# Keys' stage of a hybrid encoder step: more places for token tiles, evictions and raw weights, in memory given up by the dynamic DMAs' reserve

## The chip, the cores and the metric

The kernel runs on one core of a Trainium2 chip. The metric is device time in microseconds (us), the median of three runs. TensorE (PE) multiplies and transposes, VectorE (DVE) and ScalarE (ACT) evict and normalise, GpSimd (POOL) takes subtractions that would load DVE, and the SP queue issues every DMA of this kernel. Each engine, SP's queue included, takes its instructions in the order in which they were written down.

## The reference

One layer of a streaming encoder on 16 meta tokens, 2048 prompt tokens and 8 x 16 sample tokens. Cut to what matters here:

```python
h = layer_norm(concat([meta, x_prompt]), ln_in_g, ln_in_b)      # the samples likewise
(g_q, g_k, g_v, g_low, g_r, d_q, d_k, d_v, i_q, i_k, i_w, d_z, m_a, m_b) = split(h @ w_in)
o_a, s_t = gla_recurrence(q, k, v, log_f, s0)                    # gated linear attention
k_i = layer_norm(i_k, idx_kn_g, idx_kn_b)                        # keys of the indexer
o_b = attend(d_q, i_q, w_i, d_k, d_v, k_i)                       # top 256 keys by index score, then softmax
merged = sigmoid(m_a + gate_b[0]) * y_a + sigmoid(m_b + gate_b[1]) * y_b
h_new = layer_norm(ALPHA * h + merged @ w_out, ln_g, ln_b)
```

The keys d_k, values d_v, index keys k_i and the final state are outputs as well.

## The kernel before

Every float32 operand of a large product is split in two halves, a rounded one (`xh`, `whi`, written by ACT) and the remainder (`xl`, `wlo`, written by DVE or POOL). `mm3` (lines 265 to 267) takes three matmuls for each of eight steps of 128 along the model width, in the order hi x hi, hi x lo, lo x hi.

**Keys' stage** (`phase_keys`) goes through 18 token tiles: the meta tokens (16 rows), 16 prompt tiles of 128 rows and one tile of samples. They lie in six pieces of three tiles. For each tile `rows_in` loads x (512 KB, line 271), `prep_x` takes the LayerNorm on DVE (statistics at line 181, two steps at line 153), stores the result to `d_h` (line 283), transposes it with eight PE instructions (line 288), splits it into `xh` and `xl` (lines 159 and 144) and, for the four pieces that have to be read again later, copies it to `xf` and stores it to `d_xt` (lines 293, 294). One tile later `keys` multiplies it with two weight blocks of 300 columns (48 matmuls), evicts K (`kd`), V (`vt`) and the index columns (`xi`), transposes the keys (line 335), splits them into `ks`, and after a `yield` normalises the index keys into `xd` and transposes them (lines 349, 350). The weights come in quarters through `raw` tiles.

**Buffers.** A tile asked for by name gets the next of its pool's places and waits until the last reader of that place is done. x has three places (pool `iqp`), the evicted tiles `kd`, `vt`, `ks`, `xf` share four places of 2 KB (pool `ev`), `xi`, `xd`, `gl` four small ones (tag `evs`), `raw` has three.

**Order.** The program does not fix the order in which an engine takes its work. A list scheduler walks the program with priorities and a timeline of its own and writes one order per engine. When a place comes free at another time on that timeline, rows change places, far from the buffer that changed too.

**Afterwards.** `project` runs three groups of pieces through the remaining columns of w_in, with index scoring (line 445) and the choice of keys on DVE beside it. `phase2` then opens its own pools in the same memory: from the left the lower end (keys of the upper half, GLA pools), from the right end attention's pools (`lg`, `v`, `kdl1`, `az`, `pts`, `sm`, `st`, `aq`, `kdl0`, `up`). A pool of phase 2 can be written when the tiles of phase 1 at the same addresses are done. Attention (logits at lines 1129 and 1130, evicted by DVE at line 1131 into `lgl` and `lgu` with the row maxima `mx` in pool `sm`; transposes at 1065; product with V at 1089) is interleaved with side work: the samples' attention (lines 1182 to 1225) and the GLA recurrence (lines 682 to 960).

The memory is bounded by the reserve that the program object keeps for dynamic DMAs. Before, it has its default size, and the kernel's own tiles begin 16512 bytes into each partition.

Of the kernel before, what the change touches and what calls it, by code (L numbers as in the profile page):

```python
# [10 lines left out]
F32 = mybir.dt.float32  # L11
# [10 lines left out]
P = 128  # L22
# [21 lines left out]
KLOW = 1040  # L44
HALF = 8
LAST = [(7, 0), (6, 2), (5, 1), (0, 1), (4, 2), (2, 1), (1, 1), (3, 0)]
NP3 = 256
EARLY = 1500
SKB = 3
# [33 lines left out]
PMAX = 3 * P  # L83
# [36 lines left out]
class Trunk:  # L120
# [108 lines left out]
        return full[META + t * P : META + (t + 1) * P, :]  # L229

    def raw(self, n):
        t = self.ws.tile([P, 2 * PMAX], F32, name="raw", bufs=3)
        return t[:, : 2 * n].rearrange("p (k c) -> p k c", k=2)

    def split_sb(self, hi, lo, src, eng=None):
# [77 lines left out]
    def keys(self, t, x, c, w1, w2):  # L313

        nc, d, c0 = self.nc, self.d, COL[t]
# [8 lines left out]
        nc.sync.dma_start(self.out_rows("k", t, 256).rearrange("t (g d) -> t g d", g=4), kd[:r, :, 0, :])  # L324
        nc.sync.dma_start(self.out_rows("v", t, 256), vt[:r])
        nc.sync.dma_start(d["v"][c0 : c0 + r, :], vt[:r])
        xi = self.ev.tile([P, 80], F32, name="xi", tag="evs", bufs=4)
        nc.scalar.copy(xi[:r, 0:64], p2[:, 212:276])
        nc.scalar.copy(xi[:r, 64:80], p2[:, 284:300])
        if t != "m":  # L330
# [10 lines left out]

        mu, rstd = self.ln_stats(self.tk, xi[:r, 0:64], 64, r)
        self.stt(xi[:r, 0:64], xi[:r, 0:64], mu, self.ing[:r], OP.subtract, OP.mult)
        xd = self.ev.tile([P, 2, 64], F32, name="xd", tag="evs", bufs=4)
        for q in range(2):
            self.stt(xd[:r, q, :], xi[:r, 0:64], rstd, self.inb[:r], OP.mult, OP.add)
        nc.sync.dma_start(self.out_rows("idx_k", t, 64), xd[:r, 0, :])
# [2 lines left out]
        nc.tensor.transpose(ps[:16, 1, :r], xi[:r, 64:80], self.ident[:r, :r])  # L350
        kc = NKEY if t == "s" else (0 if t == "m" else META + t * P)
        self.split(self.kih[:, kc : kc + r], self.kil[:, kc : kc + r], ps[:, 0, :r])
        gl = self.ev.tile([16, P], F32, name="gl", tag="evs", bufs=4)
        nc.scalar.copy(gl[:, :r], ps[:16, 1, :r])
        nc.sync.dma_start(d["gl"][:, c0 : c0 + r], gl[:, :r])

# [203 lines left out]
    def phase1(self):  # L560
        nc, tc, i = self.nc, self.tc, self.i
        with ExitStack() as c:
            top = tc.tile_pool(name="top", bufs=1, side="right")
            top = c.enter_context(top)
            kp = c.enter_context(tc.tile_pool(name="kp", bufs=1))
            self.scp = c.enter_context(tc.tile_pool(name="scp", bufs=4))
            self.iqp = c.enter_context(tc.tile_pool(name="iqp", bufs=3))
            self.tk = c.enter_context(tc.tile_pool(name="tk", bufs=4))
            self.jk = c.enter_context(tc.tile_pool(name="jk", bufs=1))
            self.xp = [c.enter_context(tc.tile_pool(name=f"xp{q}", bufs=1)) for q in range(3)]  # L570
            self.ev = c.enter_context(tc.tile_pool(name="ev", bufs=4))
            self.ws = c.enter_context(tc.tile_pool(name="ws", bufs=2))
            self.pi = c.enter_context(tc.tile_pool(name="pi", bufs=4, space=PSUM))
            self.pp = c.enter_context(tc.tile_pool(name="pp", bufs=4, space=PSUM))
            self.kih = kp.tile([P, NKEY + P], F32R, name="kih")
            self.kil = kp.tile([P, NKEY + P], F32R, name="kil")
            self.iw = kp.tile([P, NT, 8], F32, name="iw")
            self.ing = self.bcast_load(kp, i["idx_kn_g"][0], 64, "ing")
            self.inb = self.bcast_load(kp, i["idx_kn_b"][0], 64, "inb")
            self.x, self.slots = {}, [0, 1, 2, 0, 1, 2, 0, 1, 2, 1]  # L580
            self.phase_keys()
            self.gng = self.bcast_load(top, i["gla_norm_g"][0], 256, "gng")
            self.gateb = top.tile([P, 16], F32, name="gateb")
            nc.sync.dma_start(self.gateb[:], i["gate_b"][0].rearrange("a (k p) -> p (a k)", p=P))
            for g in range(len(GROUPS)):
                self.project(g)
# [669 lines left out]
    def phase2(self):  # L1256
        nc, tc, d = self.nc, self.tc, self.d
        with ExitStack() as main:
# [63 lines left out]
            next(steps)  # L1322
            for j, n in LAST:
                for _ in self.attend(j):
# [165 lines left out]
```

## Time and profile before

| what | value |
|---|---|
| median of three runs | 3597.57 us (3590.15 to 3598.61) |
| profiled execution | 3593.96 us |
| its span on the core | 3592.2 us |
| PE, DVE, ACT, POOL busy in the span | 3483.6, 2528.4, 1450.9, 1088.8 us |
| DMA | 457.77 MB, mean 127 GB/s |

The span is the time from the first to the last instruction of the profiled execution. Busy times of engines overlap. In the rows further down, an instruction's idle time before it stands in square brackets, with the instruction or the DMA that ended it, and the granted clock is a share of full speed: at 1.00 PE runs at 2.4 GHz.

### The profile page before, as it was taken

How to read it: one execution, taken by the hardware profiler on the slowest of the kernel's cores; microseconds unless marked ns; L12 is line 12 of the kernel's file. 1: busy time of each engine (PE TensorE's matmuls, PEld its weight loads, DVE VectorE, ACT ScalarE, POOL GpSimd, SP SyncE). 2: the span in 40 equal slices, each digit the busy share in tenths (PEclk: the TensorE clock that was granted, in tenths of full speed). 3: DMA queues.
4: the chain of work that ended last, by engine and by line, in shares of the span. 5: the costliest groups of instructions: out<-in, count | busy, mean ns of one | idle time of the engine just before them, and what ended most of it. 6: DMA issues, size and time to landing. Idle time of an engine off the chain costs nothing. (4 is left out here: it accounts for less than half of the span.)

```text
span 3592.2 us, 66024 instructions
## 1 busy us (share of the span) xinstructions
PE 3483.6 (97%) x24196; PEld 3212.5 (89%) x24196; DVE 2528.4 (70%) x5813; ACT 1450.9 (40%) x3092; POOL 1088.8 (30%) x1412
## 2 busy tenths in 40 slices
PE   7999999999999998999999999999999999989999
PEld 6999999999999998998887788888877888879998
DVE  7737998799999998964436677676765666544444
ACT  4435223433324323322535556566565344331110
POOL 3122242242342334434411345455410000022221
PEclk9999999999999999999999999999999999999999
DMA  8642443254442345445573433333343345564431
GB/s 265 202 131 82 139 121 108 83 157 127 119 145 73 103 134 148 140 134 159 171 199 94 122 109 97 102 105 99 100 121 88 89 120 135 151 192 136 124 115 62
DMA packets 550340, 457.77 MB, mean 127 GB/s; under 512 B 95248, under 2 KB 522528, under 8 KB 550016
## 3 DMA queue, kind: packets, MB, share of 16 engines
q1 hardware_dynamic: 550016, 453.56, 43.9%
q8 instruction: 190, 3.11, 0.4%
q14 instruction: 134, 1.10, 0.1%
HBM read 292.49 MB, written 160.92 MB: 126 GB/s over the span
## 5 line engine op out<-in xcount | busy, mean ns | idle before, releaser
L144 POOL TENSOR_TENSOR wlo<-raw,whi 128x512 fp32r<-128x512 f32 x360 | 482.3, 1360 | 817.1 <-ACT whi L159 706.7
L150 DVE TENSOR_SCALAR_CACHE_REDUCE junk<-sc,cand 128x272 bf16<-128x272 f32 (+6 forms) x512 | 701.6, 1370 | 16.9
L265 PE MATMUL pp<-whi,xh 128*128 128x256 f32 (+3 forms) x1952 | 562.1, 288 | 3.5 <-ACT whi L159 2.3
L265 PE MATMUL pp<-xh,whi 128*128 128x384 f32 (+2 forms) x1728 | 563.6, 326 | 1.9 <-ACT whi L159 1.1
L267 PE MATMUL pp<-whi,xl 128*128 128x256 f32 (+3 forms) x1952 | 560.8, 288 | 4.4 <-DVE xl L144 4.4
L267 PE MATMUL pp<-xh,wlo 128*128 128x384 f32 (+2 forms) x1728 | 563.0, 327 | 1.0 <-POOL wlo L144 1.0
L266 PE MATMUL pp<-xl,whi 128*128 128x384 f32 (+2 forms) x1728 | 563.4, 326 | 0.0
L266 PE MATMUL pp<-wlo,xh 128*128 128x256 f32 (+3 forms) x1952 | 561.9, 288 | 0.0
L265 PEld LDWEIGHTS pp<-whi,xh 128*128 128x128 f32 (+1 forms) x1952 | 371.9, 191 | 12.7 <-issue 4.3
L267 PEld LDWEIGHTS pp<-whi,xl 128*128 128x128 f32 (+1 forms) x1952 | 371.0, 190 | 11.3 <-DVE xl L144 6.9
L266 PEld LDWEIGHTS pp<-wlo,xh 128*128 128x128 f32 (+1 forms) x1952 | 371.5, 190 | 7.8 <-issue 5.2
L1131 DVE CUSTOM_DVE_ANT_0 lgl<-pl,mkl 128x348 f32<-128x348 f32 (+8 forms) x608 | 296.1, 510 | 102.8 <-PE pl L1130 65.8
L265 PE MATMUL pd<-xh,wh 128*128 128x242 f32 (+3 forms) x1152 | 327.7, 285 | 8.2 <-ACT wh L1347 4.5
L159 ACT CAST whi<-raw 128x512 fp32r<-128x512 f32 (+1 forms) x344 | 199.2, 622 | 319.7 <-DMA raw<-in_w_in 204.8
L265 PEld LDWEIGHTS pp<-xh,whi 128*128 128x128 f32 x1728 | 325.1, 188 | 3.3 <-ACT whi L159 1.7
L267 PEld LDWEIGHTS pp<-xh,wlo 128*128 128x128 f32 x1728 | 324.8, 188 | 2.5 <-POOL wlo L144 1.8
L266 PE MATMUL pd<-xl,wh 128*128 128x242 f32 (+3 forms) x1152 | 324.6, 282 | 2.1 <-DVE xl L144 2.1
L266 PEld LDWEIGHTS pp<-xl,whi 128*128 128x128 f32 x1728 | 325.1, 188 | 0.6
L267 PE MATMUL pd<-xh,wl 128*128 128x242 f32 (+3 forms) x1152 | 324.5, 282 | 0.8 <-POOL wl L144 0.8
L156 ACT ACTIVATE lgl<-lgl,mx 128x1040 f32<-128x1040 f32 (+7 forms) x256 | 249.9, 976 | 177.9 <-DVE mx L1133 171.4
L1129 PE MATMUL pl<-kd,q 128*128 128x348 f32 (+14 forms) x800 | 302.5, 381 | 14.1 <-DVE mx L1131 4.9
L1130 PE MATMUL pl<-kd,q 128*128 128x348 f32 (+14 forms) x800 | 261.7, 330 | 0.0
(252 smaller groups left out, 7592.7 us busy)
## 6 DMA issues: line engine op xcount, KB each, us to landing
raw<-in_w_in SPq DMA_DIRECT2D x360, 256.0 KB, 3.2
q<-d_q SPq DMA_DIRECT2D x272, 128.0 KB, 3.0
d_h<-x SPq DMA_DIRECT2D x17, 512.0 KB, 3.3
d_gv<-en SPq DMA_DIRECT2D x68, 128.0 KB, 1.9
d_gr<-en SPq DMA_DIRECT2D x68, 128.0 KB, 2.0
d_z<-en SPq DMA_DIRECT2D x68, 128.0 KB, 1.7
v<-d_gv SPq DMA_DIRECT2D x17, 512.0 KB, 3.7
gr<-d_gr SPq DMA_DIRECT2D x17, 512.0 KB, 3.6
```

The lines of the kernel that those rows point to most:

```text
L144: (eng or self.nc.vector).tensor_tensor(out, a, b, op=op)
L150: (eng or self.nc.vector).tensor_scalar(out, a, s1, s2, op0=op0, op1=op1, **kw)
L156: self.nc.scalar.activation(out, a, f, **kw)
L159: (self.nc.vector.tensor_copy if self.spare else self.nc.scalar.copy)(out, src)
L265: mm(ps, ah(k), bh(k), start=k == 0, stop=False)
L266: mm(ps, ah(k), bl(k), start=False, stop=False)
L267: mm(ps, al(k), bh(k), start=False, stop=k == n - 1)
L1129: nc.tensor.matmul(ps[:, :m], q[:, u, :], kd, start=True, stop=False)
L1130: nc.tensor.matmul(ps[:, :m], q[:, 2 + u, :], kd, start=False, stop=True)
L1131: nc.vector.tensor_tensor_reduce(lg[z1][:, a : a + m], ps[:, :m], mk[z1][:, a : a + m], 1.0, NEG, OP.add, OP.max, mx[:, s : s + 1])
```

## The change

The reserve of the dynamic DMAs is set to 1024 bytes, and the tiles of the kernel begin 15360 bytes earlier. The room is used in phase 1: pool `iqp` has four places for x (4 KB more), `ev` seven in place of four (6 KB), the tag `evs` eight in place of four (2 KB), and `raw` four in place of three (3 KB). No instruction is added or removed; on every engine the same instructions stand in another order.

```diff
+DMA_SCRATCH = 1024
@@ raw
-        t = self.ws.tile([P, 2 * PMAX], F32, name="raw", bufs=3)
+        t = self.ws.tile([P, 2 * PMAX], F32, name="raw", bufs=4)
@@ keys
-        xi = self.ev.tile([P, 80], F32, name="xi", tag="evs", bufs=4)
+        xi = self.ev.tile([P, 80], F32, name="xi", tag="evs", bufs=8)
-        xd = self.ev.tile([P, 2, 64], F32, name="xd", tag="evs", bufs=4)
+        xd = self.ev.tile([P, 2, 64], F32, name="xd", tag="evs", bufs=8)
-        gl = self.ev.tile([16, P], F32, name="gl", tag="evs", bufs=4)
+        gl = self.ev.tile([16, P], F32, name="gl", tag="evs", bufs=8)
@@ phase1
-            self.iqp = c.enter_context(tc.tile_pool(name="iqp", bufs=3))
+            self.iqp = c.enter_context(tc.tile_pool(name="iqp", bufs=4))
-            self.ev = c.enter_context(tc.tile_pool(name="ev", bufs=4))
+            self.ev = c.enter_context(tc.tile_pool(name="ev", bufs=7))
@@ kernel
-    nc = bacc.Bacc("TRN2", target_bir_lowering=False, num_devices=1)
+    nc = bacc.Bacc("TRN2", target_bir_lowering=False, num_devices=1, dynamic_dma_scratch_size=DMA_SCRATCH)
```

In the order rows below, lines of the changed kernel are one higher than those of the profile. The first place is SP's queue at the start of the kernel. Before (a number tells the tiles of one name apart):

```order
L256 DMA raw_165<-in_w_in 128x2x300
L256 DMA raw_169<-in_w_in 128x2x300
L256 DMA raw_173<-in_w_in 128x2x300
L271 DMA x_338<-in_x_prompt 128x1024
L190 DMA gng_2373<-in_gla_norm_g 128x256
L584 DMA gateb_2375<-in_gate_b 128x16x1
L271 DMA x_462<-in_x_prompt 128x1024
L283 DMA d_h_75<-x_159 128x1024
L256 DMA raw_177<-in_w_in 128x2x300
L256 DMA raw_183<-in_w_in 128x2x212
```

And in the changed kernel, from the same row on:

```order
L257 DMA raw_165<-in_w_in 128x2x300
L257 DMA raw_169<-in_w_in 128x2x300
L257 DMA raw_173<-in_w_in 128x2x300
L257 DMA raw_177<-in_w_in 128x2x300
L272 DMA x_338<-in_x_prompt 128x1024
L272 DMA x_462<-in_x_prompt 128x1024
L191 DMA gng_2373<-in_gla_norm_g 128x256
L585 DMA gateb_2375<-in_gate_b 128x16x1
L272 DMA x_584<-in_x_prompt 128x1024
L284 DMA d_h_75<-x_159 128x1024
L257 DMA raw_183<-in_w_in 128x2x212
```

The fourth quarter of the first weight block (raw_177) and one more x tile stand ahead of the first row that waits for a place; the x loads after that stand about one tile earlier throughout the stage.

The second place is DVE ahead of the meta tile's `xd`. Before:

```order
L153 SCALAR_TENSOR_TENSOR x_584<-x_584,mv_589,lnb_156 128x1024
L181 BN_STATS st_708<-x_706 128x6
L183 BN_AGGR mv_443<-st_441 16x2
L183 BN_AGGR mv_711<-st_708 128x2
L148 TENSOR_SCALAR mv_443<-mv_443 16x1
L153 SCALAR_TENSOR_TENSOR xi_326<-xi_326,mv_443,ing_151 16x64
L148 TENSOR_SCALAR mv_711<-mv_711 128x1
L153 SCALAR_TENSOR_TENSOR x_706<-x_706,mv_711,lng_155 128x1024
L181 BN_STATS st_565<-xi_428 128x6
L144 TENSOR_TENSOR ks_437<-pk_432,ks_437 64x512
L183 BN_AGGR mv_567<-st_565 128x2
L153 SCALAR_TENSOR_TENSOR xd_448<-xi_326,mv_443,inb_153 16x64 x2
```

After (st_832, the statistics of x_830, stands two rows above the first of these):

```order
L154 SCALAR_TENSOR_TENSOR x_706<-x_706,mv_711,lng_155 128x1024
L184 BN_AGGR mv_443<-st_441 16x2
L184 BN_AGGR mv_835<-st_832 128x2
L182 BN_STATS st_565<-xi_428 128x6
L154 SCALAR_TENSOR_TENSOR x_706<-x_706,mv_711,lnb_156 128x1024
L149 TENSOR_SCALAR mv_443<-mv_443 16x1
L154 SCALAR_TENSOR_TENSOR xi_326<-xi_326,mv_443,ing_151 16x64
L149 TENSOR_SCALAR mv_835<-mv_835 128x1
L154 SCALAR_TENSOR_TENSOR x_830<-x_830,mv_835,lng_155 128x1024
L184 BN_AGGR mv_567<-st_565 128x2
L145 TENSOR_TENSOR ks_437<-pk_432,ks_437 64x512
L154 SCALAR_TENSOR_TENSOR xd_448<-xi_326,mv_443,inb_153 16x64 x2
```

The statistics and the first step of x_830 and the second step of x_706 now stand ahead of xd_448.

The third place is the handover from the projections to attention. PE before, from the last keys of the samples on (kd_21349 is the first half of the lower keys, kd_20308 an upper one):

```order
L1182 MATMUL pg<-ident,kn 128x128 x4
L1129 MATMUL pl<-kd_21349,q 128x348
L1130 MATMUL pl<-kd_21349,q 128x348
L1129 MATMUL pl<-kd_21349,q 128x348
L1130 MATMUL pl<-kd_21349,q 128x348
L1129 MATMUL pl<-kd_21349,q 128x344
L1130 MATMUL pl<-kd_21349,q 128x344
L1182 MATMUL pg<-ident,kn 128x128 x4
L1129 MATMUL pl<-kd_20308,q 128x512
L1130 MATMUL pl<-kd_20308,q 128x512
```

PE after:

```order
L1130 MATMUL pl<-kd_21349,q 128x344
L1131 MATMUL pl<-kd_21349,q 128x344
L1205 MATMUL pg<-ident,slg 128x128
L1210 MATMUL pg<-ident,slg 16x128
L1205 MATMUL pg<-ident,slg 128x128 x3
L1210 MATMUL pg<-ident,slg 16x128
L1217 MATMUL pg<-vn,pn 128x128
L1219 MATMUL pg<-vb,spt 128x128 x2
L1217 MATMUL pg<-vn,pn 128x128
L1219 MATMUL pg<-vb,spt 128x128 x2
L1225 MATMUL pg<-ident,on 128x128
L1183 MATMUL pg<-ident,kn 128x128 x8
```

After the third pair of logits PE now takes the rest of one block of sample attention and then a whole second one before the first logits with kd_20308. DVE there, after:

```order
L1195 ISA slg,smx<-pg,smk 128x272
L1195 ISA smx 128x1
L1161 CAST qsl<-q 128x4x32
L1161 CAST qsh<-q 128x4x32
L1161 CAST qsl<-q 128x4x32
L149 TENSOR_SCALAR smx<-smx 128x2
L1199 RECIPROCAL smx<-smx 128x2
L145 TENSOR_TENSOR zs<-zg,smx 128x128
L1132 ISA lgl,mx<-pl,mkl 128x348
```

The last of these rows is DVE's first logit; before, that row stood ahead of the split of the next sample keys. On SP the load of kd_21349 stood before in one place with that of kd_21351, just ahead of the last two query stores; now it stands eight rows further ahead, and kd_21351 where both were. In memory, kdl0 (the place of kd_21349) lay over pools xp1 and xp2 and lies over xp2 alone, which holds the piece whose last matmuls come first; pool sm lay over xp2 and lies over the fourth and fifth eviction places.

## Rows read from the trace of the kernel before

**Rows 1.** The page: busy us, share of the span and instructions, by engine.

```profile
PE 3483.6 (97%) x24196; PEld 3212.5 (89%) x24196; DVE 2528.4 (70%) x5813; ACT 1450.9 (40%) x3092; POOL 1088.8 (30%) x1412
```

**Rows 2.** Stretches: length; PE, PEld, DVE, ACT, POOL busy (instructions); PE's clock; DMA share; GB/s.

```profile
12.50:50.00 37.50, 31.99 (x199) 27.79 (x200) 31.35 (x55) 16.85 (x43) 13.58 (x11) 0.91 0.91 260
50.00:140.00 90.00, 83.74 (x614) 80.47 (x613) 73.67 (x160) 43.73 (x134) 23.76 (x24) 1.00 0.85 259
140.00:150.00 10.00, 10.00 (x79) 9.98 (x77) 8.12 (x20) 4.15 (x16) 1.98 (x2) 1.00 0.79 244
...
1850.00:1950.00 100.00, 87.76 (x577) 70.50 (x576) 57.38 (x195) 51.88 (x107) 16.64 (x32) 0.95 0.53 142
1950.00:2700.00 750.00, 732.10 (x5066) 608.15 (x5065) 520.52 (x1847) 445.38 (x960) 323.83 (x627) 1.00 0.38 107
```

**Rows 3.** Waits of PE, 0 to 170 us: total us, times, longest us.

```profile
PE pt L288 <- DVE x L153: 12.5, 1, 12.5
PE pp L267 <- DVE xl L144: 4.4, 6, 1.2
PE pk L349 <- DVE xd L153: 3.2, 1, 3.2
PE pp L265 <- ACT whi L159: 2.3, 2, 1.4
PE pp L265 <- ACT xh L159: 1.0, 4, 0.2
PE pk L335 <- DVE ks L144: 0.9, 1, 0.9
```

**Rows 4.** Groups of DVE, 50 to 140 us: busy us, mean ns | idle before, releaser.

```profile
L153 DVE SCALAR_TENSOR_TENSOR x<-x,mv,lnb 128x1024 f32<-128x1024 f32 x10 | 13.2, 1316 | 0.9 <-POOL mv L144 0.7
...
L181 DVE BATCH_NORM_STATS2 st<-x 128x6 f32<-128x512 f32 x20 | 12.8, 684 | 10.0 <-DMA x<-in_x_prompt 10.0
L153 DVE SCALAR_TENSOR_TENSOR x<-x,mv,lng 128x1024 f32<-128x1024 f32 x10 | 12.8, 1276 | 0.0
```

**Rows 5.** Waits of SP's queue, 0 to 170 us, at line 271 (x loads).

```profile
SPq L271 <- PE pp L267: 7.2, 4, 2.0
...
SPq L271 <- DVE x L153: 5.2, 1, 5.2
```

**Rows 6.** PE in order of time: start us, duration us, instruction, idle before.

```profile
22.35 0.45 PE L266 MATMUL pp<-wlo,xh 128*128 128x300 f32 x1
22.60 0.45 PE L267 MATMUL pp<-whi,xl 128*128 128x300 f32 x1
...
26.05 0.30 PE L266 MATMUL pp<-wlo,xh 128*16 128x300 f32 x1
26.18 0.30 PE L267 MATMUL pp<-whi,xl 128*16 128x300 f32 x1
...
45.88 1.97 PE L288 MATMUL pt<-ident,x 128*128 128x128 f32 x8
...
54.36 1.04 PE L288 MATMUL pt<-ident,x 128*128 128x128 f32 x8
```

**Rows 7.** The page: DMA queue and kind, packets, MB, share of 16 engines.

```profile
q1 hardware_dynamic: 550016, 453.56, 43.9%
```

**Rows 8.** PE at the handover, in order of time.

```profile
1860.53 0.48 PE L1216 MATMUL pg<-vn,pn 16*128 16x128 f32 x2 [0.82 <-ACT pn L1211]
...
1863.49 0.30 PE L1224 MATMUL pg<-ident,on 128*128 128x128 f32 x1 [0.78 <-DVE on L144]
...
1866.89 0.66 PE L1129 MATMUL pl<-kd,q 128*128 128x348 f32 x1 [2.62 <-DMA kd<-d_kd]
```

**Rows 9.** SP's queue at the handover: the loads of the lower keys.

```profile
1859.09 0.89 SPq L172 DMA_DIRECT2D kd<-d_kd  x2
```

**Rows 10.** ACT at the handover: keys split and softmax of a sample block.

```profile
1864.31 0.59 ACT L1184 CAST ks<-pg 128x512 fp32r<-128x512 f32 x1 [0.22 <-PE pg L1182]
...
1878.43 0.50 ACT L156 ACTIVATE slg<-slg,smx 128x272 f32<-128x272 f32 x1
```

**Rows 11.** Waits of PE, 1950 to 2700 us, the largest: total, times, longest us.

```profile
PE pg L754 <- DVE og L153: 3.3, 7, 0.9
```

## Prediction

> **What bounds the kernel now.** I read the engine line of the page first: TensorE (PE) is busy for 3483.6 of 3592.2 us [rows 1]. So only about 109 us of waiting can be won anywhere, and the question is how much of it lies where the change acts. The table by stage [rows 2] answers that. In it I subtract PE's busy time from the width of each stretch. Keys' stage runs from PE's first instruction at 12.5 us to about 140 us; from there on PE has 10.00 us of work in 10, since projection matmuls fill every gap. PE loses 37.5 - 31.99 = 5.5 us there before 50 us and 90 - 83.74 = 6.3 us after it. Two other places matter below: 12.2 us in 1850 to 1950 (the handover from projections to attention) and 17.9 us in the 750 us of attention that follow. The first reading is therefore that the whole of Keys' stage can give back 11.8 us of idle PE, a third of a percent, before anything is said about what the change does.
>
> Next, the waits of PE in that stage [rows 3]. The 12.5 us ahead of the first transpose are not touched. The 3.2 us for xd and the 2.3 us for whi are the whole loss before 50 us. The 4.4 us for xl stand for most of the loss after it, with 1.0 for xh and 0.9 for ks beside them. Then VectorE (DVE) [rows 4], because xl and xd are DVE's: in 50 to 140 us its longest idle time is 10.0 us in front of the LayerNorm statistics, waiting for the load of x. Those loads are issued late because the SP queue stands at line 271 until an x place is free [rows 5]. That is the wait that a fourth x place removes.
>
> There is a second, smaller loss: the clock. The table grants 0.91 before 50 us [rows 2]. A 300-column matmul follows its predecessor after 0.25 us at 22.35 us and after 0.13 to 0.14 us at 26 us, and eight transposes take 1.97 us right after the 3.2 us wait and 1.04 us later [rows 6]. Eleven matmuls and eight transposes and about five matmuls more at the low level cost 11 x 0.11 + 0.93 + 5 x 0.11 = 2.7 us.
>
> **The change part by part.** *The reserve.* All 550016 data packets of this kernel are in queue q1, marked hardware_dynamic, beside two small queues of instruction fetches [rows 7], and all its issues are SP's. I cost the smaller reserve at 0. The Trainium skill (DMA: Bandwidth & Descriptors, section SWDGE vs HWDGE vs iDMA) says why it should be so: the rings in that carveout hold descriptors that GpSimd writes, and transfers issued by SP or ACT never touch them. No run here shows a cut reserve yet. If the reserve mattered all the same, transfers would slow in every stage, which is the last case below.
>
> *Four raw tiles.* The fourth quarter of the first weight goes out ahead of the first waiting row (first order piece). This takes away the 2.3 us for whi. But PE then only reaches the xd wait sooner, and xd is on DVE's time. So this term is 0 by itself, and no stall of this kind is left later.
>
> *Four x places, before 50 us.* In the new order DVE does four things more ahead of xd (second order piece): two halves of statistics for a further tile, its first normalising step, and the second step of the tile before: 2 x 0.684 + 1.276 + 1.316 = 4.0 us [rows 4]. DVE idles 37.5 - 31.35 = 6.15 us in that stretch [rows 2]. If all of this idle time closes, xd comes 2.2 us sooner; if none does, 4.0 us later. I take 0.5 us sooner, since most of DVE's early waits are for loads and casts that come sooner too, but not all. The clock after the wait stays low, so the 2.7 us stay.
>
> *Four x places, after 50 us.* DVE enters this stretch about one tile ahead, and its 10.0 us of waiting for x go. DVE has 73.7 us of work there and PE 83.7, so PE is what remains, and xl, late by at most 1.2 us each time, comes in time. The 6.3 us can all go; they stay if the DMA engines, busy 0.85 of that stretch, deliver no earlier. I take 5.0. The Trainium skill (Perfetto Trace Analysis, section Identifying the Most-Contended Engine) wants weight-load busy time instead of matmul busy time for PE's headroom; by that column of rows 2 the loss is 90 - 80.47 = 9.5 us, and the sum below would be 3 us lower. I keep the matmul column, since the waits of rows 3 add up to it.
>
> *Seven eviction and eight small places.* They remove ACT's waits for places whose stores are still out. ACT is busy 43.7 of 90 us there, so this costs or gains nothing on its own: 0.
>
> Keys' stage: 0.5 + 5.0 = 5.5 us gained, from 4.0 lost to 2.2 + 6.3 = 8.5 gained.
>
> *The handover.* The pools move in memory. The first half of the lower keys (kd) now lies only over the x piece that is finished first, and its load moves ahead of the last query stores. PE's 2.6 us wait for it [rows 8, 9] can go. But the attention's row maxima (mx) now lie over eviction places, and DVE's first logit row stands behind two whole blocks of sample attention; on PE three pairs of logits are followed by those two blocks (third place). A block is a chain PE, ACT, DVE, PE with nothing of PE's between. Two links show their price now: 0.82 and 0.78 us [rows 8]. The other two (keys split, softmax) were covered by projections; their ACT steps alone take 0.59 and 2 x 0.50 us [rows 10]. At 0.6 to 1.5 us a link, eight links cost 5 to 12 us, against the 12.2 us that PE loses in these 100 us now, 4.2 of them in the three rows shown. With those three gone, and the chains in their place, this is 1 us lost to 8 us lost; if the remaining 8 us of waits for logits shrink as well, as much as 3 us are gained. I take 2 us lost.
>
> *Attention.* The GLA side work stands about 85 rows (some 12.6 us at 5066 PE instructions in 750 us [rows 2]) earlier among the logits, and no work is added. The largest PE wait for GLA is 3.3 us in 7 times [rows 11]. I take 0, from 4 gained to 10 lost. *The projections and index scoring* between Keys' stage and the handover keep their order nearly whole and have no wait for raw, iq or ev of note: 0.
>
> Sum: 3594.0 us (the profiled execution, span and launch) - 5.5 + 2.0 = 3590.5. The median of the three runs is 3597.6, so the profiled one is 3.6 us below it, well inside their spread of 8.5 us. I predict 3591 us.
>
> **The rivals.** *Everything in Keys' stage goes.* The startup waits vanish with the rest: 5.5 + 2.7 + 6.3 = 14.5 us, and the kd wait 2.6: 3594 - 17 = 3577 us. For it: DVE has idle time enough in total. Against it: the xd order of DVE, and DMA at a share of 0.91 before 50 us.
>
> *Loads are no earlier.* The transfers are issued a tile sooner but land when they did, since the engines are full; PE keeps its 11.8 us: 3594 + 2 = 3596 us. For it: the shares 0.91 and 0.85. Against it: before 13 us SP waits with the third tile's load until a place is free [rows 5], and two loads of half a megabyte move ahead of that point.
>
> *Slower: GLA ahead of its operands.* PE takes its rows in order. If each of the 16 GLA chunks now meets one more wait of 0.9 us, the longest of rows 11, attention loses 14.4 us, and with a handover at 8 us lost the time is 3594 - 5.5 + 22.4 = 3611 us. It decides from about 20 us lost. For it: all four engines have moved rows there. Against it: producers moved along with PE, and PE waits only 17.9 us in 750 now.
>
> *The reserve matters.* If it held descriptors for SP's queue, stores and loads would queue up everywhere and the time would pass 3611 too; rows 7 and the small chance of a surprise leave this 0.02, counted with the slower case.
>
> **How the numbers follow.** A measurement of this kernel can tell about 0.3% (10.8 us) from no change: faster means under 3586.8 us, slower over 3608.4 us. Forecast 0.52, everything goes 0.24, no earlier 0.15, slower 0.09 (the reserve included). Of the forecast, 0.06 lies under 3586.8 by its own bounds. So faster 0.30, same 0.61, slower 0.09. The range runs from 3578 us (about a tenth, inside the first rival) to 3603 us (the forecast with handover and attention near their slow ends).
>
> **What would show it.** Right: in 50 to 140 us DVE's wait for x falls from 10.0 us to under 2, PE's for xl from 4.4 to under 1, and a tile takes 8.2 to 8.5 us, not 9.0. The wait for whi goes, that for xd stays at 2 to 6 us. Around the end of the projections the kd wait is gone and waits for spt, pn, on and ks stand in its place, 6 to 10 us in all. Wrong: an xd wait near zero (the first rival), x loads that still hold up DVE (the second), or more than 25 us of PE waiting in attention (the third).

## The result, and the profile after

The changed kernel takes 3618.11 us (median of five, 3612.1 to 3628.9) against 3592.58 us of before on the same chip: a ratio of 1.0069, 95% interval 1.0046 to 1.0092. A later comparison gave 1.0064 (1.0051 to 1.0077). By the medians it is 25.5 us slower, 23.3 in the later comparison (r15, below); the forecast was no change, and 3618 us lies outside its range. The profiled execution took 3613.28 us with a span of 3610.7 us.

The engine line of the page, as [rows 1]. PE's busy time has grown by 8.9 us with the same instructions, so a part of the loss is no waiting at all:

```profile
PE 3492.5 (97%) x24196; PEld 3218.2 (89%) x24196; DVE 2539.7 (70%) x5813; ACT 1446.5 (40%) x3092; POOL 1084.2 (30%) x1412
```

The stretches of the changed kernel, with the columns of [rows 2]:

```profile
12.50:50.00 37.50, 27.98 (x176) 23.93 (x176) 32.04 (x53) 15.92 (x38) 19.23 (x13) 0.95 0.97 279
50.00:140.00 90.00, 88.59 (x651) 87.50 (x652) 76.62 (x174) 44.88 (x140) 21.73 (x24) 0.97 0.87 269
...
1850.00:1950.00 100.00, 85.78 (x524) 68.69 (x525) 54.65 (x193) 51.35 (x106) 16.16 (x32) 0.91 0.54 144
1950.00:2700.00 750.00, 727.10 (x5029) 602.16 (x5025) 516.62 (x1808) 436.32 (x942) 323.04 (x624) 0.99 0.38 106
```

Before 50 us PE is busy 4.0 us less than in [rows 2]; from 50 to 140 us its idle time has fallen from 6.3 to 1.4 us. In 1850 to 1950 us it runs 524 matmuls where before ran 577, nearly as busy, at a clock of 0.91 in place of 0.95. In part these are other matmuls (see below).

The largest waits of PE from 0 to 170 us, as [rows 3]:

```profile
PE pt L289 <- DVE x L154: 12.5, 1, 12.5
PE pk L350 <- DVE xd L154: 4.1, 1, 4.1
PE pp L266 <- ACT xi L330: 3.4, 1, 3.4
PE pp L266 <- ACT whi L160: 1.7, 1, 1.7
PE pp L268 <- DVE xl L145: 1.0, 2, 0.8
```

And DVE's group of statistics from 50 to 140 us, as [rows 4], its wait for x down from 10.0 to 3.1 us:

```profile
L182 DVE BATCH_NORM_STATS2 st<-x 128x6 f32<-128x512 f32 x20 | 13.0, 684 | 3.2 <-DMA x<-in_x_prompt 3.1
```

At the handover (waits of PE, 1840 to 1960 us) the wait for kd of [rows 8] is gone. A load of queries, which the prediction did not have, and the links of the sample blocks stand in its place:

```profile
PE pl L1130 <- DMA q<-d_q: 4.3, 1, 4.3
PE pg L1205 <- ACT slg L157: 2.1, 1, 2.1
PE pg L1217 <- ACT pn L1212: 1.6, 2, 0.9
...
PE pg L1225 <- DVE on L145: 1.0, 2, 0.8
...
PE pg L1193 <- DVE ks L145: 1.0, 2, 0.8
```

**Where the time went.** All kernels here run the same 24196 matmuls, so the end of the n-th matmul in a trace can be set against the end of the n-th in the trace of before. The table gives by how many us a kernel is late (negative: ahead) at the matmul that before ends at the time in the heading. Run r4, further down, has before's order unchanged: its row of lags shows how far two executions of one order can differ, up to 7 us in the middle and 2 at the end. Where two orders differ, the first n matmuls are in part others: at 1950 us 24 of those that the changed kernel has done are not those of before (50 in r2), at 1812 us 4, and none at the other times of the table. Lags are clean only where there are none.

| kernel | 50 | 165 | 997 | 1812 | 1950 | 2782 | 3550 us |
|---|---|---|---|---|---|---|---|
| changed | 5.6 | -2.1 | 5.8 | -2.4 | 7.8 | 15.1 | 18.6 |
| changed, again (r15) | 6.4 | -0.7 | 7.0 | 5.1 | 15.7 | 22.7 | 24.9 |
| r4 reserve alone | 2.2 | 2.5 | 7.1 | 4.0 | 3.2 | 1.1 | 2.4 |
| r3 fourth x alone | 7.0 | 3.6 | 3.6 | -1.5 | 0.4 | 1.7 | 4.7 |
| r5 eviction places, old attention | 1.4 | -4.5 | -5.5 | -2.1 | -6.3 | -5.7 | -0.9 |
| r13 fourth raw alone | 1.2 | 1.4 | 6.8 | 0.2 | 4.8 | 5.2 | 4.8 |
| r1 all places, old attention | 6.7 | -0.6 | 8.4 | 4.7 | 6.8 | 7.2 | 10.5 |
| r6 eviction places, new attention | 2.5 | -2.8 | -3.4 | -1.9 | 3.9 | 16.5 | 18.9 |
| r2 eviction places, third order | 0.5 | -5.5 | 0.5 | -2.5 | 10.0 | 22.9 | 26.0 |

In the changed kernel Keys' stage wins 2.1 us in all. About 5 us are lost between 910 and 997 us, 10 between 1812 and 1950 us, 7 more by 2782 us and 3.6 in the last stage. The 8 us won between 997 and 1812 us are mostly chance: r15, the same kernel, wins 2 there.

### The profile page after: what moved, and what is told of

The parts are those of the page before. It is cut to its first block, busy times and chain, and to the rows that moved or that the text cites. A ratio compares the mean times of both kernels' runs of the same rounds, so it can differ in the third digit from the quotient of the medians.

```text
span 3610.7 us, 66097 instructions
## 1 busy us (share of the span) xinstructions
PE 3492.5 (97%) x24196; PEld 3218.2 (89%) x24196; DVE 2539.7 (70%) x5813; ACT 1446.5 (40%) x3092; POOL 1084.2 (30%) x1412
## 5 line engine op out<-in xcount | busy, mean ns | idle before, releaser
L1130 PE MATMUL pl<-kd,q 128*128 128x348 f32 (+14 forms) x800 | 304.1, 383 | 12.6 <-DMA q<-d_q 8.6
L1138 POOL COPY pmeta<-lgl 128x48 f32<-128x48 f32 x256 | 58.3, 228 | 685.7 <-ACT lgl L157 628.7
```

Source lines behind the costliest of these rows:

```text
L1130: nc.tensor.matmul(ps[:, :m], q[:, u, :], kd, start=True, stop=False)
L1138: nc.gpsimd.tensor_copy(pmeta[:, h0 % 4 + u, :, g % 2, :], lg[0][:, None, 0:META].to_broadcast([P, 3, META]))
```

## The experiments

The theories were: A, the new order of handover and attention makes the loss; B, the new order of the projections does; C, any order with more stops costs clock; D, the smaller reserve itself slows transfers. The order of attention can be steered without touching the rest: an unused tile ahead of some of attention's pools moves these to other addresses, over other tiles of phase 1. Places that are not named have their number of before. "Bare rows" are the sample-attention matmuls and transposes that stand on PE in one run with nothing else between them, by the written order.

| run | bare rows | median us | before us | ratio (95%) |
|---|---|---|---|---|
| r1 all places, old attention | 20 | 3605.79 | 3596.64 | 1.0025 (1.0015-1.0034) |
| r2 ev 7, third order | 70 | 3622.55 | 3596.64 | 1.0076 (1.0059-1.0094) |
| r3 x 4, addresses kept | 17 | 3594.29 | 3596.64 | 1.0000 (0.9990-1.0010) |
| r4 reserve alone | 17 | 3597.00 | 3596.64 | 0.9999 (0.9986-1.0011) |
| r5 ev 7, old attention | 17 | 3590.99 | 3595.92 | 0.9989 (0.9976-1.0002) |
| r6 ev 7, new attention | 35 | 3612.59 | 3595.92 | 1.0046 (1.0030-1.0062) |
| r7 all but x 4, old attention | 20 | 3600.26 | 3595.92 | 1.0008 (0.9994-1.0021) |
| r8 all but raw 4, old attention | 17 | 3592.28 | 3595.92 | 0.9987 (0.9973-1.0000) |
| r9 ev 7, old attention and tail | 17 | 3584.51 | 3589.99 | 0.9986 (0.9977-0.9996) |
| r10 all but raw 4, old attention and tail | 17 | 3583.86 | 3589.99 | 0.9984 (0.9975-0.9993) |
| r11 ev 7, fourth order | 58 | 3601.38 | 3589.99 | 1.0027 (1.0016-1.0039) |
| r12 all places, kdl0 moved back | 20 | 3602.97 | 3589.99 | 1.0037 (1.0023-1.0050) |
| r13 raw 4 alone, old attention and tail | 20 | 3601.13 | 3590.20 | 1.0033 (1.0021-1.0046) |
| r14 all but raw 4 | 35 | 3603.59 | 3590.20 | 1.0039 (1.0026-1.0053) |
| r15 changed kernel | 41 | 3613.46 | 3590.20 | 1.0064 (1.0051-1.0077) |

### r4: the reserve by itself

```diff
+        ctx.enter_context(self.tc.tile_pool(name="gap", bufs=1)).tile([P, 3840], F32, name="gap")
         cp = ctx.enter_context(self.tc.tile_pool(name="cp", bufs=1))
```

> The reserve of 1024 bytes alone, with an unused tile of 15360 bytes in its place, so that every tile has the address that it had before and every engine the order of before. It asks for the price of the reserve by itself. Theories A, B and C: within 3 us of before, the spread of a median of five. Theory D: 10 us slower or more, in every stage.

0.9999: theory D falls. In this kernel, whose data all go through SP's queue, the smaller reserve costs nothing that could be measured. That agrees with what the prediction cites from the Trainium skill (DMA: Bandwidth & Descriptors, section SWDGE vs HWDGE vs iDMA): transfers issued by SP do not use the rings of descriptors that this reserve holds. What the cut reserve does to the time, it does through addresses.

### r1 and r2: the two halves of the loss

r1 is the changed kernel with a gap; r2 has only the seven eviction places (the tag evs is back at 4 too) and no gap.

```diff
 r1:
             lower = [None, right("kdl1")]
+            right("gap").tile([P, 2816], F32, name="gap")
             self.az, self.pts, self.sm = right("az"), right("pts", PTB), right("sm", 2)
 r2:
-        t = self.ws.tile([P, 2 * PMAX], F32, name="raw", bufs=4)
+        t = self.ws.tile([P, 2 * PMAX], F32, name="raw", bufs=3)
...
-            self.iqp = c.enter_context(tc.tile_pool(name="iqp", bufs=4))
+            self.iqp = c.enter_context(tc.tile_pool(name="iqp", bufs=3))
```

> The whole change, with one unused gap of 11264 bytes ahead of attention's pools of phase 2, so that az, pts, sm, st, aq, kdl0 and up lie over the same x pieces and eviction places as before. Keys' stage and the projections then run in the order of the changed kernel, handover and attention in the order of before. Theory A (the loss is made by the new order of handover and attention, which the moved pools cause): PE's lead of about 2.4 us at 1812 us stays to the end, 2 to 6 us faster than before, near 3589 us. Theory B (the loss comes from the new order of the projections, whose stalls and lower clock are carried on): about 10 us slower than before or more. Theory C (any new order with more stops lowers the clock, wherever it stands): about half of the 21 us that the changed kernel lost, 8 to 12 us slower. Theory D (the smaller reserve itself slows transfers): 20 us slower, as the changed kernel.

> Of the change only the reserve of 1024 bytes and the seven eviction places; x, raw and the small places as before. Keys' stage differs from before in a few rows, the projections not at all up to the last of them, and handover and attention have the changed kernel's order, row for row. Theory A: slower than before by what the changed kernel lost after 1812 us, 8 us at the handover and some 12 us behind it, 16 to 22 us in all, with the loss beginning at about 1850 us. Theory B: within 3 us of before. Theory C: 8 to 12 us slower, the low clock in attention alone. Theory D: about 20 us slower, but spread over all stages, from the first on.

r1 loses 9 us with attention as before: theory A alone is not enough. r2 loses 26 us with projections as before: nor is B. Theory C is not separated from them by any run: waits and low clock grow together wherever the order got worse (next section). One sentence of r2's expectation is wrong: its attention has a third order, neither that of before nor that of the changed kernel. That made it the clearest look at the handover. Stretches of r2 (first three rows) and of before (last row), columns as in [rows 2]:

```profile
1850.00:1860.00 10.00, 9.13 (x58) 8.43 (x56) 3.00 (x10) 2.95 (x8) 0.00 (x0) 1.00 0.83 248
1860.00:1890.00 30.00, 22.61 (x84) 17.68 (x84) 10.59 (x40) 7.82 (x21) 0.53 (x1) 0.50 0.85 236
...
1895.00:1950.00 55.00, 53.63 (x336) 41.60 (x337) 41.88 (x139) 33.56 (x64) 15.86 (x30) 1.00 0.36 100
```

```profile
1860.00:1890.00 30.00, 23.71 (x123) 19.37 (x123) 18.19 (x72) 14.07 (x31) 0.79 (x4) 0.83 0.72 218
```

For 30 us PE's clock stands at 0.50, the 1.2 GHz level: PE is about as busy as before in that stretch and does 84 instructions in place of 123. The run of bare rows fills the stretch, and its links are short. The waits of PE in r2, 1840 to 1960 us:

```profile
PE pg L1205 <- ACT slg L157: 3.2, 2, 1.8
PE pg L1217 <- ACT pn L1212: 2.4, 3, 0.9
PE pg L1225 <- DVE on L145: 1.5, 2, 0.8
PE pg L1193 <- DVE ks L145: 1.1, 2, 0.6
```

Between the matmuls that before ends at 1850 and 1950 us, r2 takes 112.6 us: 9.9 idle and 102.7 busy, against 12.2 idle and 87.8 busy. PE waits 2.3 us less there and is busy 14.9 us more. Not all of that is the clock: 50 of r2's 574 matmuls there are others, in the main larger ones of GLA (lines 947, 948 and 954 of before). The clock's part is an estimate from its records: 30.7 us at the half level in place of 10.2, some 10 us at half a us lost for each. In the changed kernel the stretch takes 109.7 us, 14.6 idle and 95.1 busy, with 17.1 us at the half level: by the same estimate 3 to 4 of its 9.7 us are the clock, 2.4 are waiting, and the rest is the other work that stands there.

### r5 and r6: attention's order alone

Both have the cut reserve and seven eviction places; they differ in the size of one gap (at the line of r1's): 3840 floats in r5, 768 in r6.

> The reserve of 1024 bytes and the seven eviction places, with a gap of 15360 bytes ahead of attention's pools, so that these lie over the same tiles of phase 1 as before. Keys' stage as in run r2, the projections and attention in the order of before (a few rows at the seam differ), and the run of sample-attention rows with nothing else of PE's between them is 17 rows long there, as before (41 in the changed kernel, 70 in run r2). If the eviction places alone shorten Keys' stage, as run r2 showed (5.5 us ahead of before at 165 us), and if the loss of run r2 is the order of attention alone: 5 to 6 us ahead at 165 us, and 2 to 6 us faster at the end, since the rows near 3000 to 3200 us, which every kernel with a cut reserve and moved pools has in another order, take some 2 us. If any change of order costs clock: no faster than before.

> As r5, but with a gap of 3072 bytes: the pools of attention then lie as in the changed kernel, and attention has that kernel's order, row for row, behind Keys' stage of r2 and the projections of before. (Run r2, of which that was expected, has a third order of attention, with a bare run of 70 sample rows.) If the order of attention makes the changed kernel's loss: 15 to 22 us slower than r5, with the same places as the changed kernel against before: about 8 at the handover, 4 near 2200, 6 between 2565 and 2782 us. If the length of the bare run of sample rows sets the loss at the handover through the clock: 10 to 17 us at the half clock there (about 10 before, 17 in the changed kernel, 31 in run r2), with no more waiting of PE than before. If the loss needed the changed kernel's projections ahead of it: within 5 us of r5.

r6 is 21.6 us slower than r5: the changed kernel's order of attention, with the same places and the same projections ahead of it. The lags between r5 and r6 open from 1850 us on, 10 us by 1950 and 22 by 2782. Over the whole trace, r6 has 94.9 us of PE's time at the half clock and r5 68.2 (summed over the clock's records): some 13 of the 22 us, at half a us lost for each, and the rest are waits.

From 1850 to 2782 us, where the matmuls of every kernel are again the same (but for five at the start in those with the fourth raw tile), the traces of all runs can be compared. Times in us:

| kernel | bare rows | length | PE idle | PE busy | half clock |
|---|---|---|---|---|---|
| before | 17 | 932.0 | 33.8 | 898.2 | 13.7 |
| ten others with before's order, but for some rows at the start | 17, 20 | 927.2-941.8 | 30.5-35.3 | 896.3-906.6 | 6.8-34.1 |
| changed | 41 | 949.1 | 42.7 | 906.3 | 30.7 |
| changed, again (r15) | 41 | 949.1 | 42.1 | 907.0 | 30.7 |
| r6 | 35 | 950.4 | 40.7 | 909.6 | 34.1 |
| r14 (below) | 35 | 949.3 | 40.8 | 908.5 | 37.5 |
| r11 (below) | 58 | 944.3 | 39.2 | 905.1 | 30.7 |
| r2 | 70 | 957.4 | 44.3 | 913.0 | 37.5 |

So the changed kernel's order costs 17 us between these points. In the changed kernel 8.9 are waits and 8.1 are busy time of the same matmuls, beside 17 us more at the half clock; in r6, r14 and r15 7 to 8 are waits and 9 to 11 busy time. The idle times of old and new orders do not overlap.

Where the waits are: the largest of PE in the changed kernel from 2574 to 2798 us,

```profile
PE px L1066 <- ACT pt L1074: 4.3, 5, 1.7
PE px L1066 <- DVE st L1076: 3.6, 2, 2.2
PE oo L1090 <- ACT pt L1074: 3.1, 2, 2.6
```

against those of before for the matmuls of the same numbers, 2565 to 2782 us:

```profile
PE pd L266 <- DVE xl L144: 2.1, 1, 2.1
PE pl L1129 <- DVE mx L1131: 2.0, 4, 0.7
PE pl L1129 <- ACT pt L1010: 1.8, 1, 1.8
```

PE now waits for ACT's and DVE's evictions (pt, st) of what it has transposed. Between the matmuls of 1950 and 2782 us such waits ahead of transposes and product with V come to 18.8 us in the changed kernel, 18.5 in r15 and 17.5 in r6, against 5.2 in before and 4.7 in r5. Why the order thins out there is not shown by any run; the second half of attention's loss is placed, not explained.

### r11: does the length of the bare run set the clock?

As r9 (below), but with the first gap ahead of kdl0 and up alone, which gives a fourth order with 58 bare rows.

> The places of r9, but with the first gap ahead of kdl0 and up alone. The scheduler then makes a fourth order of attention, in which 58 rows of sample attention stand on PE with nothing else between them (17 before, 41 in the changed kernel, 70 in r2). If the length of the bare run sets the handover's loss through the clock: 20 to 28 us at the half clock in one stretch near 1870 us and 8 to 13 us lost between 1850 and 1950 us; and if such an order also thins out the work that covers attention's waits later, 15 to 25 us slower than r9 in all. If the losses of r2 and r6 are peculiar to their orders: any value, half clock of 10 us or less.

The half clock lasts 23.9 and 3.4 us near 1860 us, and the matmuls that before ends from 1850 to 1950 us (43 of them others) take 111.6 us in place of 100.0, 12.8 of them idle: as expected for the handover. In all it is 16.9 us slower than r9, near the low end. The stretch, as r2's second row:

```profile
1860.00:1890.00 30.00, 23.34 (x97) 18.20 (x97) 14.08 (x54) 9.52 (x23) 0.75 (x2) 0.62 0.83 227
```

Time at the half clock around the handover against the bare rows, over all kernels: 3 to 20 us with 17 or 20 rows, 10 to 17 with 35 or 41, 27 with 58, 31 with 70. So a long run goes with a long half clock at 58 and 70 rows; up to 41 rows, as in the changed kernel, the ranges overlap, and the length of the run is not shown to be its cause there.

### r12: one tile

```diff
             self.st, self.aq = right("st"), right("aq", 2)
+            right("gap").tile([P, 2816], F32, name="gap")
             lower[0] = right("kdl0")
...
             pool = lambda n, bufs=1, **kw: c.enter_context(tc.tile_pool(name=n, bufs=bufs, **kw))
+            pool("gapf").tile([P, 3840], F32, name="gapf")
             cp, wk, pp = pool("fc"), pool("fk", FKB), pool("fo", 4, space=PSUM)
```

> The whole change with all its places, and two gaps: 11264 bytes ahead of kdl0 (the first half of the lower keys) and up, every other pool of attention staying where the changed kernel has it, and 15360 bytes ahead of fc. Attention and the last stage then have the order of before row for row, so it asks whether the place of that one tile makes the changed kernel's loss in attention. If it does: 12 to 17 us faster than the changed kernel, 5 to 7 us slower than before (r1 lost 9, of which the tail gives 3 back), and what is left is the projections' loss of r1. If the other pools' places matter too: less.

With only kdl0 and up moved by 11264 bytes, every engine has r1's order up to the last stage; with up alone moved, the order that the scheduler writes is the changed kernel's (the order only; it was not run). So it is kdl0, the first half of the lower keys, whose place decides. From 1950 us to the end r12's lag grows by 2.7 us, the changed kernel's by 10.8. In all r12 is 13 us slower than before, 10 us better than r15: less than the 12 to 17 us expected, but the intervals of r1 and r12 overlap. In its trace it loses 7 us by 997 us, and 8 at the handover, where its bare run is 20 rows and its half clock 20.4 us. r1 has the same order there and lost 2 us, with 13.7 us at the half clock: one trace's handover is worth some 6 us of chance.

### r3, r7, r8: which place does what in Keys' stage

r3 cuts the reserve by the 4096 bytes of the x tile and nothing else (`DMA_SCRATCH = 12288`); r7 and r8 are the changed kernel less one place, with the gap of r5 and of r1.

> The fourth x place alone, with the reserve cut by exactly the 4096 bytes that it takes, so that all pools behind it keep their addresses. Keys' stage has a new order, the projections move in parts, handover and attention keep before's order. It asks how much of Keys' stage the x place is worth without the other places. If the x place is what shortened Keys' stage in the changed kernel (2.5 us ahead at 165 us): 2 to 3 us ahead there and 2 to 4 us faster at the end. If the eviction places were needed for it: under 1 us ahead. Theory A: nothing is lost afterwards. Theory B or C: the parts of the projections that moved take 3 us or more back before 1850 us.

> The changed kernel with three x places, and attention in the order of before by a gap of 15360 bytes. Run r1 lost 6.5 us before 50 us and won 7.3 us after it. If the fourth x place makes the early loss (two x loads and a weight quarter compete ahead of the meta tile's chain): 0 to 2 us late at 50 us and about 5 ahead at 165. If the fourth raw tile makes it: 5 us or more late at 50 us, as r1. The stop of index scoring between 923 and 997 us (6 us in r1 and in the changed kernel, not in r2 and r3) should be there if the fourth raw tile moves the projections, since the order of these is nearly r1's.

> The changed kernel with three raw tiles, and attention in the order of before by a gap of 11264 bytes. If the fourth x place makes the loss before 50 us: 5 to 7 us late at 50 us, and level with before or up to 1 us ahead at 165. If the raw tile makes it: 5 us ahead at 165 us. The stop between 923 and 997 us should be gone (0 to 1 us), if it comes with the fourth raw tile. At the end: within 3 us of before, against 9 us slower in r1.

r3 met neither of its two cases for Keys' stage: it is 3.6 us late at 165 us. Every kernel with the fourth x place is 5.6 to 7.5 us late at 50 us; those without it are 2.5 us late at most, r7 and r13 with the fourth raw tile among them. The third tile's transposes begin at 51 to 52 us in place of 46. So x makes the early loss, as r7 and r8 were to tell. With the x place and three raw tiles (r3, r8, r10, r14) PE's wait for DVE ahead of the transposes of xd is 7.4 to 8.2 us long (3.2 in before), and those for whi sum to 3.0 to 4.5.

After 50 us both kinds of place win, the eviction places more. Between the matmuls that before ends at 50 and 165 us, r3 wins 3.5 us, the eviction places alone (r2, r5, r6, r9, r11) 5.4 to 7.0, and both together 5.8 to 7.8, so the x place adds little to the others. With the eviction places alone PE is 2.8 to 7.9 us ahead at 165 us. ACT and DVE from 50 to 140 us: two rows of before, two of r3, one of r9:

```profile
ACT vt L321 <- DMA d_kd<-ks: 5.6, 4, 2.7
DVE st L181 <- DMA x<-in_x_prompt: 10.0, 5, 2.8
```

```profile
ACT vt L322 <- DMA d_kd<-ks: 6.7, 5, 2.4
DVE st L182 <- DMA x<-in_x_prompt: 9.0, 5, 2.5
```

```profile
DVE st L182 <- DMA x<-in_x_prompt: 5.8, 6, 2.1
```

With a fourth x place DVE still waits 9.0 us for x. With seven eviction places ACT's wait for the keys' stores has gone, and DVE's for x falls to 5.8 us without any further x place. SP's queue issues in its written order, with stores of what ACT evicts ahead of x loads, and they go out sooner when ACT does not wait. That this is the way from the one to the other is argued from these rows; no run tried it by itself.

r8's stop between 923 and 997 us is gone (0 us), r7 has it (6.8 us), as expected.

### r13 and r14: the fourth raw tile

r13 has only the raw tile, with both gaps of r9; r14 is the changed kernel with `name="raw", bufs=3`; r15 the changed kernel beside them.

> The fourth raw tile alone (three x, four eviction, four small places), reserve 1024, and the two gaps of r9, so that attention and the last stage keep the order of before. If the raw tile by itself makes the projections' loss: about 6 us lost between 923 and 997 us and 2 to 3 between 1133 and 1206, 7 to 14 us slower than before at the end (r1 less r8 gives 13.7, r7 less r5 gives 7). If the loss needs the x places beside it: within 4 us of before.

> The changed kernel with three raw tiles and nothing else altered: attention has the changed kernel's order (a bare run of 35 sample rows, 41 there), the projections nearly that of before. If the two causes add up: slower than before by r6's 16 us, within 3 us, and 8 to 12 us faster than the changed kernel. If attention's order alone makes the loss: as the changed kernel.

> The changed kernel itself, beside r13 and r14, to compare with on the same runs of before. Its first five runs gave 1.0069 (1.0046 to 1.0092). If the causes add up (raw tile 7 to 14, attention's order 20, Keys' stage and the rest -5): 22 to 29 us slower than before, 1.006 to 1.008.

The raw tile alone costs 10.9 us, and taking it out of the changed kernel gives 9.9 back. By their lags all six kernels with it lose 5.4 to 7.4 us between 923 and 997 us, and the ten others 0.1 us at most. At 923 us 18 matmuls of the six are others. Between 910 and 1206 us, where the first n matmuls are the same, they lose 5.5 to 6.8 us, the others 2.2 at most; in the changed kernel 3.4 of 5.8 are waits and 2.4 busy time, with 6.8 us at the half clock where before has none. The traces do not show where the rest of the 10.9 us is lost. Waits of PE and of ACT there, in r13 (910 to 1007 us) and in before (910 to 1000 us):

```profile
PE pi L446 <- ACT rl L157: 5.5, 4, 2.4
ACT rl L157 <- DVE sc L154: 24.7, 14, 4.7
```

```profile
PE pi L445 <- ACT rl L156: 2.1, 3, 1.0
ACT rl L156 <- DVE sc L153: 19.4, 14, 3.0
```

PE waits for rl of index scoring, and rl for the sum sc on DVE. DVE is what is full in this part: busy 700.85 of 750 us in before from 600 to 1350 us,

```profile
600.00:1350.00 750.00, 740.97 (x4772) 732.46 (x4771) 700.85 (x1087) 277.71 (x555) 250.87 (x201) 1.00 0.40 118
```

so it has little room to catch up a row that it takes later; that this is why the new order loses here is argued, not tried. The causes add up: raw tile 10.9, changed kernel without it 13.4, together 24.3 us; r15 lost 23.3. In turn, the changed kernel without the raw tile and without attention's new order (r8) is 3.6 us faster than before, and that order costs the 17 us between r8 and r14.

### r9 and r10: the better version

Seven eviction places alone (r9), or with the x and small places too (r10), attention's order kept by the gap ahead of az, and the gap ahead of fc of r12.

> As r5 (seven eviction places and the cut reserve, attention in the order of before), with a second gap of 15360 bytes ahead of pool fc of the last stage, so that its tiles lie where they lay before; the rows near 3000 to 3200 us, in another order in every kernel so far but r4, are then in before's order too. If that order costs the 3 to 4 us that those kernels lost between 2967 and 3246 us: 7 to 9 us faster than before, 2 to 4 us faster than r5. If these 3 us are chance: as r5, 5 us faster than before.

> As r8 (the changed kernel with three raw tiles and attention in the order of before), with the second gap of r9. With the tail's 3 us back: 6 to 8 us faster than before. If the tail's loss is chance: as r8, 4 us faster. It also says which is worth more, the eviction places alone (r9) or with the x and small places beside them; by the leads at 165 us (4.5 in r5, 0 in r8) r9 should be faster by up to 4 us.

Both beat before, by 5.5 and 6.1 us (0.9986 and 0.9984), and so the changed kernel too; that is less than the 0.3% that one measurement of three runs could tell. The second gap's 3 us are not seen in the times: r9 against r5 and r10 against r8 differ by 0.0003. In the traces they are: between 2967 and 3246 us every kernel without that gap but r4 loses 2.0 to 4.6 us, those with it (r9 to r13) 1.1 at most. r9 misses its first case (7 to 9 us), r10 lies at the edge of its own (6 to 8), and the 4 us that r9 should have over r10 are not borne out.

## Why the prediction was wrong

*The bound, and the size of Keys' stage after 50 us.* Right in direction: the idle time fell from 6.3 to 1.4 us, DVE's x wait to 3.1 (forecast under 2), xl to 1.0, and PE's tile takes about 8.2 us there. The size was off: from 5.6 us late to 2.1 ahead are 7.7 us won, where 5.0 were forecast and 6.3 at most. Busy time of the same matmuls fell too, by 2.5 us, and idle PE is no bound on that. By the weight-load column, which the prediction weighed and set aside, 9.5 us of loss after 50 us fell to 2.5. Of the signs named, the tile's time and xd came true, x and xl nearly, and whi did not go (1.7 us).

*Before 50 us: 0.5 gained was forecast, 5.6 were lost.* The bounds were 4.0 lost and 2.2 gained, from DVE's order ahead of xd. The xd wait is 4.1 us, inside its forecast; what came new is 3.4 us for xi, ACT's. ACT's row for xi stood behind two casts of whi that had waited 2.9 and 1.0 us for their loads. The step counted only DVE's rows and not ACT's behind the loads. With the x place but three raw tiles the xd wait is 7.4 to 8.2 us, over 4 us longer than in before, so the step's worst case for DVE's rows was the nearer one; which of the waits the x place lengthens depends on the raw tiles beside it. Net, Keys' stage won 2.1 us and not 5.5.

*Who wins it.* The prediction gave the x place the whole gain and the eviction places 0. The runs show nearly the reverse: at 165 us the x place alone is 3.6 us late (r3), the eviction places alone are 2.8 to 7.9 ahead (r5 and others). The load that waits for a place stood in [rows 5], but DVE's wait did not end with that place (9.0 us in r3).

*"The projections keep their order nearly whole": this step failed, 10.9 us.* The fourth raw tile alone (r13) moved the projections' order: if PE's order is cut in twenty equal parts, eight of the parts that hold projections have another row in 17 to 51% of their places. The term was put at 0 because that order was taken to be kept and the stage shows no wait for raw; a place that removes no wait still moved the order of another stage, where DVE has 6.6% of slack.

*The handover and attention: 2 us lost and 0 were forecast; these steps failed, by 15 us.* From 1850 to 2782 us the changed kernel loses 17 us, 8.9 waiting and 8.1 in busy time. At the handover the waits were sized well: 14.6 us of idle time in place of 12.2, kd gone, the links shown above 5.7 us in all (6 to 10 forecast), the longest 2.1; the 4.3 us for queries were not foreseen. What the term left out is the clock, which [rows 2] already showed at 0.95 in that stretch and which the same text had priced in Keys' stage: over the 932 us the half level lasts 30.7 us in place of 13.7.

The step for attention said 0, from 4 gained to 10 lost, because no work is added. The rows that cover a wait had moved: the waits for pt and st grew from 5.2 to 18.8 us while others shrank. The rival named GLA as what would wait. That its time of 3611 us came near the measured one is luck: the rows that wait are others. The sign of more than 25 us of waiting was set too high: it is 22.9 us from 1950 to 2700, in place of 17.9. How the 17 us fall to the two steps one trace cannot tell: at 1950 us the orders have done different matmuls.

*The last stage.* The sum has no term for it, though its pools moved as well. Between 2967 and 3246 us the changed kernel lost 3.6 us and r15 2.0; with the gap of r9 to r13 it is 1.1 at most.

*The gain that was a cost.* The prediction counted 2.6 us for the keys' load that can start earlier, because kdl0 lies over one x piece and no longer over two. That wait was indeed gone on the chip, but the same move was the origin of attention's loss: r12 shows that the place of this very tile gives attention its new order.

*The reserve: 0.* Right (r4), and the rival of the reserve falls.

## What to carry to other kernels

Where a scheduler lays out later pools over earlier ones, freed memory is not neutral: moving one tile over another owner can change the order of a whole later stage, and that is worth more than the waits that the freed memory removes. Before such a change is timed as a whole, its places should be tried one at a time with the later pools pinned to the tiles they lay over; here the eviction places helped, the x and small places together changed nothing in the end (r9, r10) and the raw tile cost 11 us. A chain of short dependent steps on TensorE is to be priced with the clock, not by its waits alone.

## What the runs showed of the hardware

PE at the half clock looks busy. In r2 it was busy 75% of 30 us at 0.50 granted, while it advanced by 84 instructions; a table of busy shares reads the loss as work. In those 30 us PE waited 0.5 to 1.8 us at a time, with some 2 to 4 us of matmuls between, and no single wait was longer; the clock was back at 1.00 in the stretch from 1895 us, where logits and transposes stand back to back. Between executions, too, the time follows the clock: the five of the changed kernel took 3612.1 and 3613.3 us at mean clocks of 0.988, and 3623.8 and 3628.9 us at 0.983.
